# A hybrid attention and ConvFFN layer on one core: when the projections' weights are loaded, when a power is taken, and in which order the kernel begins

## The chip, the core and the metric

The kernel runs on one core of a Trainium2 chip. Its five instruction streams are those of TensorE (PE), VectorE (DVE), ScalarE (ACT), GpSimd (POOL) and SyncE (SP, which here only issues DMAs). Each takes its instructions in program order and waits on semaphores of the others. ACT issues a few DMAs of its own. The metric is device time in microseconds (us); the median of three runs is shown for the kernel before.

## What is computed

One layer over 1024 latent tokens and 256 context tokens of 1024 channels. Cut to what the change touches:

```python
mod = jax.nn.silu(c) @ w_mod[l] + b_mod[l]
shift1, scale1, gate1, shift2, scale2, gate2 = jnp.split(mod[:, None, :], N_MOD, axis=-1)
...
h = x * (1.0 + scale1) + shift1
...
proj = h @ w_in + b_in                   # q, k, v of two attentions, and 2048 gate columns
q_b = _rope_2d(_qk_rms(q_b, q_norm_g))   # t * (mean(t * t) + eps) ** -0.5 * g, then rotary
...
g_a, g_b = jnp.split(jax.nn.sigmoid(gate_logits), 2, axis=-1)
```

Behind this follow a windowed and a global attention, their merge, a layer norm, a convolutional feed-forward part and a second layer norm. The change leaves those as they are.

## The kernel before

**Arithmetic.** Every operand of a product is split into a high part (rounded to the type fp32r) and a low part (what rounding lost), and each product is three passes of PE: high by high, high by low, low by high (`mm3`, lines 88 to 91). A high part is a copy, on ACT as a rule (line 81, CAST in the trace); a low part is a subtraction, on DVE or POOL (line 86).

**The beginning (lines 199 to 278).** c is loaded as a row into all partitions (`spread_load`, 64 partitions on ACT's queue, 64 on SP's), and ACT takes its silu (`spread`, line 184). For each of eight channel tiles k, `load1` loads two 512 KB tiles of the transposed modulation weights (wm, for shift and scale), a raw 256 KB weight tile of the global queries (wr) and a 512 KB tile of x; line 192 (`mod`) multiplies wm by silu(c) and sums it on DVE, which gives a column of shift or scale. `modulate` then makes hh and hl, the parts of h, on ACT (lines 230 and 231, twice the same affine function) and DVE (line 237), and splits the next raw weights. PE multiplies tile k into eight accumulators, q1acc, in 24 products of 512 columns (lines 275 to 278). In each cycle of loads the raw weights come ahead of x.

**The rest of the projections (lines 656 to 832).** An order is written out by hand (GORD): 3 gates, the group qa (windowed queries of tokens 0 to 511), 4 gates, qb (the other tokens), 4 gates, ka (keys and values), 1 gate, kb, 4 gates. A gate is 48 products for 128 gate columns in two halves; a group runs over eight k, each with its own weight tile (12 products per k in qa and qb, 15 in ka and kb). The weights pass through three raw buffers (tile raw, RAWB): `fetch_raw` issues a load for each buffer counted free, `prefetch` splits them one step ahead, and in `prefetch` the last call is `fetch_raw` (lines 688 and 699), so raw loads are issued directly behind the splits that free the buffers. A load waits at the head of SP's queue until its buffer is really free, and what is behind it on SP waits as well.

Beside this, `mods` (line 718) spreads 48 more products of modulation rows over the half gates and the k steps: `fetch` issues the load of a row (wml0, wml1, ..., 512 KB, on SP) and line 192 multiplies it on DVE. The rows have a ring of four buffers (WRING), so the load of row n waits for the product of row n - 4.

`side_step` runs the queries' normalisation (`qpost`) in steps, one per half gate: s1 (a rotary table on POOL, squares on ACT), s1b (sums on DVE, line 330; then the power -0.5 on POOL, line 332, and its negative, line 370), an empty step (GAP), and s2 (rotary, lines 304 to 312, on DVE or POOL). The power's results pqs and nqs are read in the attention.

Up to the start of ka the order of all five streams is that of the program (`manual_schedule`, closed at line 785); from there on a scheduler orders them, and it also lifts a few small loads into the earlier part of SP's queue.

The rest of the kernel runs over 32 attention units, the merge, and the feed-forward part; PE is kept supplied there by orders and delays that the change does not touch.

Of the kernel before, what the change touches and what calls it, by code (L numbers as in the profile page):

```python
# [17 lines left out]
KT = 8  # L18
# [38 lines left out]
UE = "vector", "vector", "vector", "vector", "vector", "gpsimd", "gpsimd"  # L57
LN2_P = 2, 2, 2
GAP = 1
WRING = 4  # L60
LN1_S = slice(0, 512), slice(512, 768), slice(768, 1024)
VOFF = 0.0
# [6 lines left out]
def layer_kernel(  # L69
# [65 lines left out]
    def hput(*names):  # L135
        for n in names:
            hfree.append(hslot.pop(n))
# [8 lines left out]
    def acc_tile(name, dt=F32):  # L146
        return ps1.tile([P, 512], dt, tag="acc", name=name)
# [28 lines left out]
    def spread_load(src, n, engs):  # L176
        rows[n] = ht(f"row{n}")
        hput(f"row{n}")
        for m, eng in enumerate(engs):
            w = P // len(engs)  # L180
            eng.dma_start(rows[n][m * w:(m + 1) * w], src.partition_broadcast(w))
# [14 lines left out]
    Q = {}  # L196
    st1 = {}

    def load1(k):
        wm = []  # L200
        for j in (0, 1):
            w = tmp(f"wm{j}_{k}")
            nc.sync.dma_start(w, wmodT[j * 8 + k])
            wm.append(w)
        x = tmp(f"xr{k}")
        wr = raw(f"wr{k}")
        nc.sync.dma_start(wr, w_qb[k])
        for s in [slice(0, HALF), slice(HALF, T)] if k == 0 else [slice(0, T)]:
            nc.sync.dma_start(x[:, s], xT[k][:, s])
        st1[k] = wm, x, wr  # L210

    def product(j, k):
        col = j * 8 + k
        mod(st1[k][0][j], sc, bmc[:, col:col + 1], modc[:, col:col + 1])

    def modulate(k):
        wr = st1[k + 1][2] if k + 1 < KT else None
        if k == 0:
            w0.append(wsplit(st1[0][2], "qb0", "gpsimd"))
        elif k + 1 < KT:  # L220
            w0.append([ph1.tile([P, 512], R32, tag="wp", name=f"w{a}qb{k + 1}", bufs=8) for a in "hl"])
            nc.scalar.copy(w0[-1][0], wr)
        product(1, k)
# [4 lines left out]
        ss = (slice(0, HALF), slice(HALF, T)) if k == 0 else (slice(0, T),)  # L228
        for s in ss:
            nc.scalar.activation(hh[:, s], x[:, s], AF.Identity, bias=a, scale=b)  # L230
            nc.scalar.activation(x[:, s], x[:, s], AF.Identity, bias=a, scale=b)
        if k + 1 < KT:
            if k:
                nc.vector.tensor_tensor(out=w0[-1][1], in0=wr, in1=w0[-1][0].bitcast(F32), op=ALU.subtract)
            product(0, k + 1)
        for s in ss:
            nc.vector.tensor_tensor(out=hl[:, s], in0=x[:, s], in1=hh[:, s].bitcast(F32), op=ALU.subtract)
        if k == 0:
            w0.append(wsplit(wr, "qb1"))
        hT.append((hh, hl))  # L240

    loads = ctx.enter_context(ExitStack())
    E = mybir.EngineType
    loads.enter_context(tc.manual_schedule(engines={E.SP, E.PE, E.DVE, E.Activation, E.Pool}))
    spread_load(c_row, 0, (nc.scalar, nc.sync))
    nc.scalar.dma_start(bmc, bmod)
    load1(0)
    spread(sc, 0)
    nc.vector.tensor_scalar(out=bmc[:, 8:16], in0=bmc[:, 8:16], scalar1=1.0, scalar2=None, op0=ALU.add)
    for k in (1, 2):  # L250
        load1(k)
    acc = [acc_tile(f"q1acc{t}") for t in range(NT)]
    w0 = []
    product(0, 0)
    modulate(0)
# [69 lines left out]
    def rms_scale(x3, H, nm, sq, ss=None, square=True):  # L325
        if square:
# [4 lines left out]
        nc.vector.tensor_scalar(out=ss, in0=ss, scalar1=1.0 / HD, scalar2=QK_EPS, op0=ALU.mult, op1=ALU.add)  # L331
        nc.gpsimd.tensor_tensor(out=ss, in0=ss, in1=mhalf[:, 0:H], op=ALU.pow)
        return ss
# [17 lines left out]
    def qpost(br, t):  # L351
        q = qtile(br, t)
        q3 = q.rearrange("p (h d) -> p h d", d=HD)
        if br == 0:
            def r0():
                rope(nc.gpsimd if t % 3 == 2 else nc.vector, q, q, 8, ropec[:, t], ropes[:, t], f"q0_{t}")
            return [r0]
        st = {}

        def s1():  # L360
            st["tb"] = ph1.tile([P, 2, HD], F32, tag="tb", name=f"tbq{t}", bufs=4)
            gfold(st["tb"], 0, t, nc.gpsimd)
            rms_square(q3, sqq[0][:, t % 2])

        def s1b():
            rms_scale(q3, 8, f"q{t}", sqq[0][:, t % 2], pqs[:, t], False)
            if t == NT - 1:
                sqq.clear()
                hput("sqq")
            nc.gpsimd.tensor_scalar(out=nqs[:, t], in0=pqs[:, t], scalar1=-1.0, scalar2=0.0, op0=ALU.mult, op1=ALU.add)  # L370

        def s2():
            tb = st["tb"]
            rope(nc.gpsimd if t % 3 == 2 else nc.vector, q, q, 8, tb[:, 0], tb[:, 1], f"q1_{t}")
        return [s1, s1b] + [lambda: None] * GAP + [s2]

    sqq = [ht("sqq", (P, 2, 512))]
    for t in range(NT):
# [302 lines left out]
    def prefetch(gi, k):  # L681
        if gi == "g":
            hs = []
            for a in (0, 1):
                hs.append(wsplit(rawt.pop((gi, k, a))[0], f"g{k}_{a}", "gpsimd"))
                raws[1] += 1
            ready[gi, k] = hs
            fetch_raw()
            return
        nm, src, tiles = groups[gi]  # L690
        wr, cx = rawt.pop((gi, k, 0))
        w, c = wsplit(wr, f"{nm}{k}"), None
        raws[1] += 1
        if cx is not None:
            nc.scalar.activation(cx, cx, AF.Identity, bias=modx[:, k:k + 1], scale=modx[:, 8 + k:9 + k])
            c = [ph1.tile([P, NC], R32, tag="ch", name=f"c{a}{k}", bufs=4) for a in "hl"]
            split(cx, *c, nc.vector, nc.vector)
        ready[gi, k] = w, c
        fetch_raw()

    late = [(col, sc, modc[:, col:col + 1]) for col in range(16, 48)]
    late += [(col, scc, modx[:, col:col + 1]) for col in range(16)]
# [80 lines left out]
    for n, (gi, k) in enumerate(order):  # L783
        if (gi, k) == (0, 0):
            loads.close()
            bias_kv = bias_tile(b_kv, "bias_kv")
        while nxt < len(order) and sum(ahead[n:nxt + 1]) <= 8:
            prefetch(*order[nxt])
            nxt += 1
        if gi == "g":  # L790
            for hf in (0, 1):
                last = gate(k, hf)
                mods(3 * KT)
                if not turn[0]:
                    prepare()
                    nc.vector.tensor_scalar(out=bias_qa, in0=bias_qa, scalar1=0.125, scalar2=None, op0=ALU.mult)
# [1039 lines left out]
```

## Time and profile before

| | us |
|---|---|
| median of three runs (lowest, highest) | 1592.48 (1592.48, 1593.41) |
| the profiled execution | 1589.56 |
| its span, first to last instruction | 1587.8 |
| PE busy | 1533.4 |
| DVE, ACT, POOL busy | 1175.5, 813.9, 728.8 |
| mean granted clock of PE | 0.994 |

The span lies 1.8 us below the profiled execution's own time. A row of a timeline reads: start (us), duration (us), engine, line, operation, out<-in, count, and in brackets the idle time of that engine just before it and what ended it. SPq and ACTq are the DMA issues of SP and ACT; a row with a count merges several instructions. Waits read: total, times, longest.

### The profile page before, as it was taken

What the parts mean: (1) busy time and instruction counts of PE and PEld (TensorE: products, weight loads), DVE (VectorE), ACT (ScalarE), POOL (GpSimd) and SP (SyncE); (2) the same over time, 40 slices, a digit from 0 to 9 for tenths busy, and PEclk for the clock granted to TensorE, in tenths of its full rate; (3) what the DMA queues carried; (4) which work ended last, traced back from release to release, by engine and by line L of the source; (5) the groups of instructions that cost most, each with busy time, mean ns of one, the idle gap of its engine ahead of it and who ended that gap; (6) DMA issues with size and microseconds to landing.
All of it is one profiled execution on the core that took longest, in us unless ns stands there. A gap on an engine that the chain in (4) does not pass through costs nothing.

```text
span 1587.8 us, 22177 instructions
## 1 busy us (share of the span) xinstructions
PE 1533.4 (97%) x7748; PEld 1276.1 (80%) x7748; DVE 1175.5 (74%) x1767; ACT 813.9 (51%) x1450; POOL 728.8 (46%) x728
## 2 busy tenths in 40 slices
PE   7999899999999999999999999999999999999997
PEld 5888688878886887777788988888888888888887
DVE  6674876628888777888674778788888787647884
ACT  5322122448887667688531564444444444435552
POOL 0254422416667556665422453566667665021121
PEclk9999999999999999999999999999999999999999
DMA  9666663322236556531451222333334446996831
GB/s 368 235 220 208 223 233 126 116 84 65 64 103 158 139 128 144 119 72 39 144 180 57 80 81 93 107 107 106 107 107 116 112 118 177 362 277 205 257 107 54
DMA packets 112528, 230.00 MB, mean 145 GB/s; under 512 B 12992, under 2 KB 27840, under 8 KB 112320
## 3 DMA queue, kind: packets, MB, share of 16 engines
q1 hardware_dynamic: 97184, 199.72, 38.1%
q0 software_dynamic: 10400, 20.19, 8.3%
q10 hardware_dynamic: 4832, 8.68, 1.5%
q8 instruction: 61, 1.00, 0.3%
q14 instruction: 51, 0.42, 0.1%
HBM read 177.35 MB, written 65.86 MB: 153 GB/s over the span
## 4 chain that ended last, share of the span: by engine, by line
PE 80%; DVE 8%; ACT 4%; DMA 3%; POOL 3%; issue 2%; SPq 0%; DVEq 0%; ACTq 0%; POOLq 0%
PE ptr L576 5%; PE p L90 4%; PE p L91 4%; PE p L89 4%; PE b L91 3%; PE b L90 3%; PE b L89 3%; PE g L89 3%; PE g L91 3%; PE g L90 3%; PE s L459 2%; PE av L597 2%; PE d L89 2%; PE c L89 2%; PE a L89 2%
## 5 line engine op out<-in xcount | busy, mean ns | idle before, releaser
L586 DVE TENSOR_TENSOR ptl<-ptr,pth 128x512 fp32r<-128x512 f32 x188 | 124.8, 685 | 27.5 <-ACT pth L585 25.3
L576 PE MATMUL ptr<-ident,p 128*128 128x128 f32 x816 | 126.7, 278 | 10.0 <-DVE ptl L586 7.7
L585 ACT CAST pth<-ptr 128x512 fp32r<-128x512 f32 x188 | 106.5, 588 | 56.1 <-PE ptr L576 32.6
L86 DVE TENSOR_TENSOR ld<-rd,hd 128x1024 fp32r<-128x1024 f32 x77 | 94.9, 1250 | 50.4 <-ACT hd L81 48.3
L471 ACT ACTIVATE p<-p,nm 128x1024 f32<-128x1024 f32 (+2 forms) x128 | 125.4, 982 | 10.8 <-DVE p L504 10.0
L576 PEld LDWEIGHTS ptr<-ident,p 128*128 128x128 f32 x816 | 93.7, 140 | 40.1 <-DVE ptl L586 13.8
L81 ACT CAST hd<-rd 128x1024 fp32r<-128x1024 f32 x77 | 79.4, 1049 | 80.7 <-PE p L91 51.7
L597 PE MATMUL av<-pth,VT 128*128 128x512 f32 x236 | 104.6, 443 | 1.0 <-ACT avs L603 0.5
L89 PE MATMUL p<-hd 128*128 128x512 f32 x264 | 103.2, 391 | 0.0
L90 PE MATMUL p<-ld,hd 128*128 128x512 f32 x264 | 102.8, 389 | 0.0
L91 PE MATMUL p<-hd,ld 128*128 128x512 f32 x264 | 102.8, 389 | 0.0
L91 PE MATMUL g<-hh,wlg 128*128 128x512 f32 x256 | 99.8, 390 | 0.8 <-POOL wlg L86 0.8
L89 PE MATMUL g<-hh,whg 128*128 128x512 f32 x256 | 99.9, 390 | 0.0
L90 PE MATMUL g<-hl,whg 128*128 128x512 f32 x256 | 99.6, 389 | 0.0
L598 PE MATMUL av<-ptl,VT 128*128 128x512 f32 x236 | 97.7, 414 | 2.0 <-POOL ptl L86 1.8
L86 POOL TENSOR_TENSOR wlg<-wg,whg 128x512 fp32r<-128x512 f32 x32 | 42.7, 1346 | 114.5 <-ACT whg L81 110.5
L504 DVE TENSOR_SCALAR_CACHE_REDUCE p<-s,cvt,nmc 128x1024 f32<-128x1024 f32 x64 | 84.5, 1340 | 12.3 <-PE s L460 12.0
L459 PE MATMUL s<-KL,q 128*128 128x512 f32 (+2 forms) x192 | 76.0, 396 | 2.7 <-ACT p_x L471 2.0
L192 DVE CUSTOM_DVE_ANT_0 wml<-wml,sc,bmc 128x1024 f32<-128x1024 f32 x32 | 44.7, 1412 | 37.5 <-DMA wml<-in_wmodT_dram 37.5
L83 POOL TENSOR_SCALAR pth<-prw 128x512 fp32r<-128x512 f32 x48 | 30.9, 643 | 88.9 <-ACT prw L582 63.1
L460 PE MATMUL s<-KL,q 128*128 128x512 f32 (+2 forms) x192 | 71.6, 373 | 0.0
L81 ACT CAST wS<-s 128x512 fp32r<-128x512 f32 x76 | 45.7, 621 | 47.2 <-POOL s L1167 44.0
(429 smaller groups left out, 4940.5 us busy)
## 6 DMA issues: line engine op xcount, KB each, us to landing
wml<-in_wmodT_dram SPq DMA_DIRECT2D x48, 512.0 KB
ru<-in_w_up_dram SPq DMA_DIRECT2D x38, 512.0 KB
rd<-td SPq DMA_DIRECT2D x55, 256.0 KB
rd<-sd SPq DMA_DIRECT2D x44, 256.0 KB
rd<-in_w_dn_dram SPq DMA_DIRECT2D x33, 256.0 KB
wm<-in_wmodT_dram SPq DMA_DIRECT2D x16, 512.0 KB
wg<-in_w_g_dram SPq DMA_DIRECT2D x32, 256.0 KB
sgd<-sg ACTq DMA_DIRECT2D x32, 256.0 KB
```

Source lines behind the costliest of these rows:

```text
L81: nc.scalar.copy(hi, src)
L86: lo_eng.tensor_tensor(out=lo, in0=src, in1=hi.bitcast(F32), op=ALU.subtract)
L89: nc.tensor.matmul(ps, a[0], b[0], start=start, stop=False, skip_group_check=resumed)
L90: nc.tensor.matmul(ps, a[0], b[1], start=False, stop=False, skip_group_check=resumed)
L91: nc.tensor.matmul(ps, a[1], b[0], start=False, stop=stop, skip_group_check=resumed)
L459: nc.tensor.matmul(o, self.q[0][:, hs], ks, start=True, stop=False)
L471: nc.scalar.activation(p, s, AF.Exp, bias=nm[:, h:h + 1], scale=scale, accum_out=sm[:, h:h + 1])
L576: nc.tensor.transpose(tr[:, h * P:(h + 1) * P], self.pslice(h, n), ident)
L585: nc.scalar.copy(hi, tr)
L586: nc.vector.tensor_tensor(out=lo, in0=tr, in1=hi.bitcast(F32), op=ALU.subtract)
L597: nc.tensor.matmul(self.av, v, hi, start=first, stop=False)
L598: nc.tensor.matmul(self.av, v, lo, start=False, stop=self.left == 0)
```

## The change

1. Raw weights in the gates: `prefetch` no longer calls `fetch_raw` at its end. In a gate the call stands behind the first half's products and `side_step`, in a k step of a group ahead of `prefetch`; where a raw tile isn't there when it is to be split, it is fetched then.
2. The power: s1b ends with the sums; the power and its negative move to a new step s1c in the place of the empty step.
3. The beginning: bmc (the modulation bias, 24 KB) is now the first load on ACT's queue and the second half of c_row the second; a silu of one column of ones (into negsink, which is set later) is put ahead of everything ACT computes, and with it the load of ACT's function table; x of tile 0 is loaded around its raw weights, and from then on raw weights are loaded one tile ahead, behind x; the high part of tile 0's weights is a copy on DVE behind the first two products, no longer on ACT; DVE takes the second product of tile 1 between the two halves of hl0; PE gets 28 products of ones, 128 by 128 by 128 in f32, into an accumulator ahead of its work.

```diff
+    def load_w(k):
+        wr1[k] = wr = raw(f"wr{k}")
+        nc.sync.dma_start(wr, w_qb[k])
...
-        wr = raw(f"wr{k}")
-        nc.sync.dma_start(wr, w_qb[k])
-        for s in [slice(0, HALF), slice(HALF, T)] if k == 0 else [slice(0, T)]:
-            nc.sync.dma_start(x[:, s], xT[k][:, s])
-        st1[k] = wm, x, wr
+        if k == 0:
+            nc.sync.dma_start(x[:, 0:HALF], xT[k][:, 0:HALF])
+            load_w(0)
+            nc.sync.dma_start(x[:, HALF:T], xT[k][:, HALF:T])
+        else:
+            nc.sync.dma_start(x, xT[k])
+        if k + 1 < KT:
+            load_w(k + 1)
+        st1[k] = wm, x
...
         if k == 0:
-            w0.append(wsplit(wr, "qb1"))
+            product(1, 0)
+            w = [ph1.tile([P, 512], R32, tag="wp", name=f"w{a}qb0", bufs=8) for a in "hl"]
+            split(wr1[0], *w, nc.vector, nc.gpsimd)
+            w0.append(w)
+            high(slice(0, HALF))
+            high(slice(HALF, T))
+            product(0, 1)
+            low(slice(0, HALF))
+            product(1, 1)
+            low(slice(HALF, T))
+            w0.append(wsplit(wr1[1], "qb1"))
...
-    spread_load(c_row, 0, (nc.scalar, nc.sync))
     nc.scalar.dma_start(bmc, bmod)
+    spread_load(c_row, 0, (nc.sync, nc.scalar))
+    nc.scalar.activation(negsink[:, 0:1], onec, AF.Silu)
     load1(0)
...
+    for _ in range(NWARM):
+        nc.tensor.matmul(acc[-1][:, 0:P], onesf, onesf, start=True, stop=True)
...
         def s1b():
-            rms_scale(q3, 8, f"q{t}", sqq[0][:, t % 2], pqs[:, t], False)
+            rms_scale(q3, 8, f"q{t}", sqq[0][:, t % 2], pqs[:, t], True)
...
+        def s1c():
+            rms_power(pqs[:, t], 8)
             nc.gpsimd.tensor_scalar(out=nqs[:, t], in0=pqs[:, t], scalar1=-1.0, scalar2=0.0, op0=ALU.mult, op1=ALU.add)
...
-        return [s1, s1b] + [lambda: None] * GAP + [s2]
+        return [s1, s1b, s1c, s2]
...
             for a in (0, 1):
+                if (gi, k, a) not in rawt:
+                    fetch_raw()
                 hs.append(wsplit(rawt.pop((gi, k, a))[0], f"g{k}_{a}", "gpsimd"))
                 raws[1] += 1
             ready[gi, k] = hs
-            fetch_raw()
             return
         nm, src, tiles = groups[gi]
+        if (gi, k, 0) not in rawt:
+            fetch_raw()
...
         ready[gi, k] = w, c
-        fetch_raw()
...
+        if gi != "g":
+            fetch_raw()
         while nxt < len(order) and sum(ahead[n:nxt + 1]) <= 8:
...
                 side_step()
+                if hf == 0:
+                    fetch_raw()
             continue
```

How the change moves instructions, at three places. First SP's queue in the last gate ahead of qb and in qb itself. wqb0 to wqb7 are the raw weights of qb's eight k steps, wml rows those of `mods`. Before:

```order
L675 DMA wqb1_1207<-in_w_qa_dram 128x512
L675 DMA wqb2_1209<-in_w_qa_dram 128x512
L714 DMA wml22_1239<-in_wmodT_dram 128x1024
L714 DMA wml23_1274<-in_wmodT_dram 128x1024
L714 DMA wml24_1277<-in_wmodT_dram 128x1024
L675 DMA wqb3_1294<-in_w_qa_dram 128x512
L675 DMA wqb4_1300<-in_w_qa_dram 128x512
L714 DMA wml25_1330<-in_wmodT_dram 128x1024
L714 DMA wml26_1333<-in_wmodT_dram 128x1024
```

And after:

```order
L751 DMA wml22_1262<-in_wmodT_dram 128x1024
L710 DMA wqb1_1272<-in_w_qa_dram 128x512
L710 DMA wqb2_1274<-in_w_qa_dram 128x512
L751 DMA wml23_1303<-in_wmodT_dram 128x1024
L751 DMA wml24_1306<-in_wmodT_dram 128x1024
L751 DMA wml25_1353<-in_wmodT_dram 128x1024
L751 DMA wml26_1356<-in_wmodT_dram 128x1024
L710 DMA wqb3_1366<-in_w_qa_dram 128x512
L710 DMA wqb4_1368<-in_w_qa_dram 128x512
```

One wml row (wml22) has moved ahead of wqb1 and wqb2, and two (wml25 and wml26) ahead of wqb3 and wqb4.

Second POOL's queue in the four gates between qa and qb. wlg5_0 is the low part of the first half of gate 5's weights, `cvt<-cvt,mhalf` the power, the TENSOR_SCALAR behind it its negative, tbq a rotary table of the query tile of that number. Before:

```order
L315 TENSOR_TENSOR tbq4_1060<-ropet_137,gcol_138 128x64
L320 TENSOR_TENSOR tbq4_1060<-ropet_137,gcol_138 128x2x16 x2
L332 TENSOR_TENSOR cvt_69<-cvt_69,mhalf_72 128x8
L370 TENSOR_SCALAR cvt_69<-cvt_69 128x8
L86 TENSOR_TENSOR wlg5_0_1106<-wg5_0_979,whg5_0_1105 128x512
L86 TENSOR_TENSOR wlg5_1_1110<-wg5_1_1022,whg5_1_1109 128x512
L315 TENSOR_TENSOR tbq5_1151<-ropet_137,gcol_138 128x64
L320 TENSOR_TENSOR tbq5_1151<-ropet_137,gcol_138 128x2x16 x2
L332 TENSOR_TENSOR cvt_69<-cvt_69,mhalf_72 128x8
L370 TENSOR_SCALAR cvt_69<-cvt_69 128x8
L86 TENSOR_TENSOR wlg6_0_1200<-wg6_0_1024,whg6_0_1199 128x512
```

And after:

```order
L343 TENSOR_TENSOR tbq4_1085<-ropet_137,gcol_138 128x64
L348 TENSOR_TENSOR tbq4_1085<-ropet_137,gcol_138 128x2x16 x2
L87 TENSOR_TENSOR wlg5_0_1133<-wg5_0_1021,whg5_0_1132 128x512
L87 TENSOR_TENSOR wlg5_1_1137<-wg5_1_1090,whg5_1_1136 128x512
L365 TENSOR_TENSOR cvt_69<-cvt_69,mhalf_72 128x8
L405 TENSOR_SCALAR cvt_69<-cvt_69 128x8
L343 TENSOR_TENSOR tbq5_1176<-ropet_137,gcol_138 128x64
L348 TENSOR_TENSOR tbq5_1176<-ropet_137,gcol_138 128x2x16 x2
L87 TENSOR_TENSOR wlg6_0_1227<-wg6_0_1092,whg6_0_1226 128x512
```

The power and its negative have moved from ahead of a gate's low parts to behind them; between the low parts of gates 5 and 6 there now stands the power of the query tile before.

Third ACT's queue at the start of the program. row0 is c's row, 64 of its partitions; whqb0 the high part of tile 0's weights. Before:

```order
L181 DMA row0_146<-in_c_row_dram 64x1024
L246 DMA bmc_61<-in_bmod_dram 128x48
L184 ACT_TABLE_LOAD
L184 ACTIVATE sc_142<-row0_146 128x1024
L81 CAST whqb0_186<-wr0_155 128x512
L230 ACTIVATE hh0_191<-xr0_154,modc_60 128x512
```

And after:

```order
L270 DMA bmc_61<-in_bmod_dram 128x48
L182 DMA row0_147<-in_c_row_dram 64x1024
L272 ACT_TABLE_LOAD
L272 ACTIVATE negsink_63<-onec_70 128x1
L185 ACTIVATE sc_142<-row0_147 128x1024
L241 ACTIVATE hh0_217<-xr0_155,modc_60 128x512
```

The two loads have changed places, the table load no longer has a row ahead of it that it must wait for, and the cast has left this queue.

More of the change, by code (lines that the diff above doesn't have):

```diff
@@ L59 @@
 GAP = 1
+NWARM = 28
 WRING = 4
@@ L197, in layer_kernel @@
     st1 = {}
+    def load_w(k):
+        wr1[k] = wr = raw(f"wr{k}")
+        nc.sync.dma_start(wr, w_qb[k])
+    wr1 = {}
     def load1(k):
@@ L216, in modulate @@
     def modulate(k):
[L217 to L223, printed above, removed]
+        last = k + 1 == KT
+        if k:
+            if not last:
+                w0.append([ph1.tile([P, 512], R32, tag="wp", name=f"w{a}qb{k + 1}", bufs=8) for a in "hl"])
+                nc.scalar.copy(w0[-1][0], wr1[k + 1])
+            if k > 1:
+                product(1, k)
         hh = hTp.tile([P, T], R32, tag="hT", name=f"hh{k}", bufs=16)
@@ L227, in modulate, with high, low @@
         x = st1[k][1]
-        ss = (slice(0, HALF), slice(HALF, T)) if k == 0 else (slice(0, T),)
-        for s in ss:
+        def high(s):
             nc.scalar.activation(hh[:, s], x[:, s], AF.Identity, bias=a, scale=b)
             nc.scalar.activation(x[:, s], x[:, s], AF.Identity, bias=a, scale=b)
[L232 to L236, printed above, removed]
+        def low(s):
             nc.vector.tensor_tensor(out=hl[:, s], in0=x[:, s], in1=hh[:, s].bitcast(F32), op=ALU.subtract)
         if k == 0:
-            w0.append(wsplit(wr, "qb1"))
+            product(1, 0)
[9 more added lines that the diff above has]
+            w0.append(wsplit(wr1[1], "qb1"))
+        else:
+            high(slice(0, T))
+            if not last:
+                nc.vector.tensor_tensor(out=w0[-1][1], in0=wr1[k + 1], in1=w0[-1][0].bitcast(F32), op=ALU.subtract)
+                product(0, k + 1)
+            low(slice(0, T))
         hT.append((hh, hl))
@@ L323, in rms_square, with rms_scale @@
         nc.scalar.activation(sq.rearrange("p (h d) -> p h d", d=HD), x3, AF.Square)
-    def rms_scale(x3, H, nm, sq, ss=None, square=True):
-        if square:
+    def rms_scale(x3, H, nm, sq, ss=None, late=False):
+        if not late:
             rms_square(x3, sq)
@@ L331, in rms_scale, with rms_power @@
         nc.vector.tensor_scalar(out=ss, in0=ss, scalar1=1.0 / HD, scalar2=QK_EPS, op0=ALU.mult, op1=ALU.add)
+        if not late:
+            rms_power(ss, H)
+        return ss
+    def rms_power(ss, H):
         nc.gpsimd.tensor_tensor(out=ss, in0=ss, in1=mhalf[:, 0:H], op=ALU.pow)
-        return ss
     def rms_apply(x3, H, ss):
```

## The prediction

> **What bounds the kernel now.** I read the page first, then the waits of TensorE (PE) over the projections (0 to 400 us), and then the timelines of the engines around the two places where those waits sit. The page:
>
> ```profile
> span 1587.8 us, 22177 instructions
> PE 1533.4 (97%) x7748; PEld 1276.1 (80%) x7748; DVE 1175.5 (74%) x1767; ACT 813.9 (51%) x1450; POOL 728.8 (46%) x728
> ```
>
> PE is busy for 97% of the span, so a change that adds no PE work can only give back time in which PE waits, or runs slowly, where the change reaches. These are the waits of PE in the first 400 us (total, times, longest):
>
> ```profile
> PE q1acc L275 <- ACT hh L230: 11.4, 2, 10.7
> PE accqb L90 <- DVE wlqb L86: 5.9, 1, 5.9
> PE g L91 <- POOL wlg L86: 0.8, 1, 0.8
> ```
>
> The reader is to see three places: the beginning (10.7 + 0.7), one stop of 5.9 in the group qb, one of 0.8 in the gate ahead of it. First the stop in qb on PE's timeline:
>
> ```profile
> 163.31 0.39 PE L89 MATMUL accqb<-whqb,hh 128*128 128x512 f32 x1
> 169.61 0.80 PE L90 MATMUL accqb<-wlqb,hh 128*128 128x512 f32 x1 [5.91 <-DVE wlqb L86]
> 170.20 0.63 PE L91 MATMUL accqb<-whqb,hl 128*128 128x512 f32 x1
> 170.62 0.63 PE L89 MATMUL accqb<-whqb,hh 128*128 128x512 f32 x1
> ...
> 174.12 0.39 PE L89 MATMUL accqb<-whqb,hh 128*128 128x512 f32 x1
> ...
> 179.56 0.39 PE L89 MATMUL accqb<-whqb,hh 128*128 128x512 f32 x1
> ```
>
> From 174.12 to 179.56 PE issues 24 products, one each 0.227 us. Behind the stop they come every 0.42 to 0.43 (170.20 to 170.62). Between 163.31 and 174.12 lie 12 issues, which at 0.227 take 2.7; they took 10.8. The stop thus costs **8.1 us**: the wait and the slow stretch behind it.
>
> Why is wlqb late? VectorE (DVE), then SyncE's queue (SP):
>
> ```profile
> 144.16 1.28 DVE L192 CUSTOM_DVE_ANT_0 wml<-wml,sc,bmc 128x1024 f32<-128x1024 f32 x1
> 164.65 1.28 DVE L192 CUSTOM_DVE_ANT_0 wml<-wml,sc,bmc 128x1024 f32<-128x1024 f32 x1 [3.67 <-DMA wml<-in_wmodT_dram]
> 168.87 1.29 DVE L86 TENSOR_TENSOR wlqb<-wqb,whqb 128x512 fp32r<-128x512 f32 x2
> ```
>
> ```profile
> 147.27 1.57 SPq L675 DMA_DIRECT2D wqb<-in_w_qa_dram  x2
> 148.94 2.49 SPq L714 DMA_DIRECT2D wml<-in_wmodT_dram  x3
> 157.31 0.93 SPq L675 DMA_DIRECT2D wqb<-in_w_qa_dram  x2
> 158.29 1.37 SPq L714 DMA_DIRECT2D wml<-in_wmodT_dram  x3
> ```
>
> DVE stood still for the row wml25, issued at 158.29; only then came its product, the rotary step and the sums (3.0 us, from the product's end at 165.9 to 168.87), and last the two splits PE was waiting for. wml25 was issued so late because wqb3 and wqb4 stood ahead of it (157.31), and those wait for a free raw buffer. The pair before them (147.27) waited for GpSimd (POOL), as did the gate that lost 0.8:
>
> ```profile
> 136.33 1.14 ACT L81 CAST whg<-wg 128x512 fp32r<-128x512 f32 x2 [0.45 <-DMA wml<-in_wmodT_dram]
> 159.23 2.08 ACT L81 CAST whqb<-wqb 128x512 fp32r<-128x512 f32 x3 [0.47 <-ACT sg L746]
> ```
>
> ```profile
> 143.13 2.60 POOL L332 TENSOR_TENSOR cvt<-cvt,mhalf 128x8 f32<-128x8 f32 x1 [11.16 <-DVE cvt L331]
> 145.98 2.52 POOL L86 TENSOR_TENSOR wlg<-wg,whg 128x512 fp32r<-128x512 f32 x2
> ```
>
> The high parts of that gate's weights were ready from 136.33 on, but in POOL's order the power stood ahead of the low parts, and it stood 11.16 us for sums on DVE.
>
> **The change, the power and the raw weights.** With the power one step later, POOL reaches the low parts of gate 6 when their high parts are there: they start by about 137.5 instead of 145.98, so the 0.8 goes, and the raw buffers that wqb1 and wqb2 need come free about 8 us sooner. In SP's new order wml25 stands ahead of wqb3 and wqb4. It then waits only for its ring buffer, which the product of wml21 frees (144.16 + 1.28 = 145.4). From issue to use wml25 took 164.65 - 158.29 = 6.4, so I put it at 152 at the latest, 12 us sooner. DVE then needs three products (3.7), the 3.0 of rotary step and sums and a few small operations moved in behind them; counted from 152 that ends near 157. The bound is then the cast at 159.23: split at about 160.4, and PE wants it at 163.5 (163.31 + 0.23). About 3 us of cover is left, and 8.1 + 0.8 = **8.9 us** come back. From both sides: nothing, if another row is as late there; 8.9, if all goes.
>
> What the change adds is that raw loads now queue behind one or two rows of wml on SP, and a row of wml waits for DVE's product four rows earlier. Behind such a wait stand raw weights, and for them ScalarE (ACT) with its casts, then PE. As the raw buffers come free no later than before, I cost this at nothing; without that cover a late raw weight would cost PE what it costs above, a few us and the slow stretch. The four small loads that SP issued among the first wml rows (bias_kv, two of cx, the conv bias) come a few rows later, ahead of a raw load that must wait for its buffer anyway: nothing. The power's own results are wanted only in the attention.
>
> **The change, the beginning.** The first 27 us:
>
> ```profile
> 0.73 0.57 ACTq L181 DMA_DIRECT2D row<-in_c_row_dram  x1
> 0.86 0.17 DVE L116 MEMSET onesf<- 128x128 f32 x1
> 1.34 0.85 ACTq L246 DMA_DIRECT2D bmc<-in_bmod_dram  x1
> 4.61 1.28 ACT L184 ACT_TABLE_LOAD   x1 [4.61 <-DMA row<-in_c_row_dram]
> 5.93 1.06 ACT L184 ACTIVATE sc<-row 128x1024 f32<-128x1024 f32 x1
> 7.16 0.17 DVE L249 TENSOR_SCALAR bmc<-bmc 128x8 f32<-128x8 f32 x1 [6.12 <-DMA bmc<-in_bmod_dram]
> 7.29 1.28 DVE L192 CUSTOM_DVE_ANT_0 wm<-wm,sc,bmc 128x1024 f32<-128x1024 f32 x1
> 9.68 1.26 POOL L86 TENSOR_TENSOR wlqb<-wr,whqb 128x512 fp32r<-128x512 f32 x1 [9.25 <-ACT whqb L81]
> 9.82 0.81 ACT L230 ACTIVATE hh<-xr,modc 128x512 fp32r<-128x512 f32 x1 [0.23 <-DVE modc L192]
> 10.69 0.79 PE L275 MATMUL q1acc<-whqb,hh 128*128 128x512 f32 x1 [10.69 <-ACT hh L230]
> ...
> 16.76 0.40 PE L275 MATMUL q1acc<-whqb,hh 128*128 128x512 f32 x1
> 18.08 0.62 ACT L222 CAST whqb<-wr 128x512 fp32r<-128x512 f32 x1 [3.89 <-DMA wr<-in_w_qb_dram]
> 19.89 0.50 PE L275 MATMUL q1acc<-whqb,hh 128*128 128x512 f32 x1 [0.70 <-ACT hh L230]
> ...
> 22.60 0.62 ACT L222 CAST whqb<-wr 128x512 fp32r<-128x512 f32 x1 [1.48 <-DMA wr<-in_w_qb_dram]
> ```
>
> ```profile
> 26.19 0.39 PE L275 MATMUL q1acc<-whqb,hh 128*128 128x512 f32 x1
> ```
>
> ```profile
> 62.55 0.41 DVE L796 TENSOR_SCALAR bias_qa<-bias_qa 128x512 f32<-128x512 f32 x1
> ```
>
> ```profile
> 1576.27 0.69 PE L1658 MATMUL zt<-pr,zz 128*128 128x128 f32 x4
> 1576.80 0.50 PE L1663 MATMUL stl<-onec,pr 128*128 128x1 f32 x4
> ```
>
> PE starts at 10.69 and runs slowly until 16.76; channel tile 1 starts at 19.89, held by the cast at 18.08, which waits for wr2 and stands ahead of hh1 on ACT; tile 2 starts at 26.19. From there on PE no longer waits in this stage, so 26.19 is what has to move.
>
> The table load leaves the path. But the second half of c_row is now issued on ACT behind bmc. As first of that queue it let ACT go on at 5.93 or just before; the second of the queue, bmc, landed at 7.16. SP's half, issued at the same time, landed at 4.61, 1.3 sooner than ACT's: that is what a half costs. So the second half, as second, lands between 4.7 (bounded below by SP's half, if bmc costs nothing) and 7.16 + 1.3 = 8.4. I take 8.4, since the place in the queue is that of bmc. Then: silu to 9.5 (1.06), the first hh 2.5 behind the start of the first product, as before (7.29 to 9.82), at 12.0, and PE's first product 0.87 behind hh (9.82 to 10.69), at 12.85. The cast of wr0 is now on DVE behind the two products (11.9), 0.41 by the nearest row: 12.3; POOL's low part 1.26: 13.6; PE's second product at 13.65. On the good side, wr2 is loaded ahead of tile 2's two 512 KB rows; a tile's 1.8 MB take 4.5 (18.08 to 22.60, the casts that wait for wr2 and wr3), so wr2 comes 2.6 sooner, at 15.5, and tile 1 no longer waits for it.
>
> The 28 products can start when onesf is set, at about 1.1. Four of that shape take 0.53 at full speed (1576.27 to 1576.80), 0.13 each, so 0.25 at the slow rate: they end between 1.1 + 3.7 and 1.1 + 7.0, by 8.1. Then PE idles for 4.7 us or more until 12.85. The wait of 5.91 above was long enough for the slow rate; I take it that this one is too. [...]
>
> Slow stretches lasted 4.5 and 6.1 here (169.61 to 174.12, 10.69 to 16.76). From 12.85 that is to 17.4 or 18.9: of the 23 products from 13.65 on, 9 to 12 take 0.42, the rest 0.227, so tile 0 ends at 20.6 to 21.3, and with tile 1's 24 x 0.227 = 5.44 the next tile begins at 26.0 to 26.7, against 26.19. I take **0** for the beginning. The other edits cost nothing: the products write an accumulator whose first real product starts it anew, and the extra silu runs while the rows load.
>
> **The sum.** 8.1 + 0.8 + 0 = 8.9. The profiled execution took 1589.56 (span 1587.8 and 1.8 around it), 2.9 below the median of 1592.48; against its own time 1589.56 - 8.9 = 1580.7, span 1578.9; against the median **1583.6**.
>
> **The rivals.**
> 1. *The beginning gains too.* The clock stays up through the gap, or c_row lands early. With the clock up: 13.65 + 23 x 0.227 = 18.9, and 24.3 for the next tile, 1.9 gained. With c_row landing as early as before as well, tile 1 is held by its loads, which come 2.6 sooner: 2.6 gained. That gives 1592.48 - 8.9 - 1.9 = 1581.7, or 1581.0. [...] Against: the queue's place of c_row. Chance 0.30.
> 2. *The stop shrinks or moves.* Less waiting on one row shows the next: a raw weight behind wml makes PE wait 2 to 6 somewhere in qa, qb or ka. Result 8.9 less 3 to 7: 1586.6 to 1590.6, mostly about 1587.5. The cover in qb is only 3 us. Chance 0.13.
> 3. *It does not do what it says.* DVE's order around wlqb is the same as before (product, rotary step, sums, splits); if its row is as late as ever, the 8.1 stays and only 0.8 goes: 1591.7. Against: the row's place on SP has changed. Chance 0.07.
> 4. *Slower.* In the first k/v group (ka), scheduled freely, the scaling of the context now stands on ACT ahead of the third cast and waits for products whose rows were pushed back on SP; if each of the six remaining weights there waits for a row (6.4 from issue to use, against 15 x 0.227 = 3.4 of PE work per weight), that is 6 x 3.0 = 18 and a slow stretch (8.1 - 5.9 = 2.2 above), so -8.9 + 20 = +11: 1603.6; it is slower as soon as more than 2 us are lost on each. Against: before, nothing in that group waited. Chance 0.05.
>
> The forecast has 0.45. **Chances:** 0.2% is about what a measurement of this kernel can tell from no change (3.2 us: 1589.3 to 1595.7). Faster: forecast, rival 1 and nearly all of rival 2: 0.87. Same: rival 3 and a little of 2: 0.08. Slower: 0.05. **Range:** forecast (-0.5 to +0.2 for the beginning), rival 1 down to 1580.0 with its last tenths, and the greater part of rival 2: 1580.0 to 1588.0; some 0.16 is left out.
>
> **What would show it.** Right: no wait of PE on wlqb or wlg above 0.5 us, no slow stretch in qb, POOL's low parts directly behind their casts, wml25 landed before DVE wants it; PE's first real product near 12.9, slow again, and tile 2 begun near 26. Wrong: PE's first product before 11 or at full speed; a wait of PE on wlqb that stays; a new wait on wqa, wka or whka; a time above 1588.

## The result and the profile after

| | before | after |
|---|---|---|
| median (lowest to highest) | 1592.24 (1590.44 to 1593.41), 6 runs | 1579.37 (1577.02 to 1581.23), 6 runs |
| profiled execution, its span | 1589.56, 1587.8 | 1578.46, 1576.7 |

The changed kernel is faster: the ratio of the times is 0.992, 95% interval 0.9907 to 0.9933. The forecast was 1583.6, its range 1580.0 to 1588.0; the result lies 4.2 below the one and 0.6 below the other. By the medians 12.9 us are gained, by the two profiled executions 11.1.

The page of after:

```profile
span 1576.7 us, 22297 instructions
PE 1538.4 (98%) x7804; PEld 1283.1 (81%) x7804; DVE 1199.0 (76%) x1768; ACT 813.8 (52%) x1450; POOL 740.2 (47%) x728
```

PE is busy for 5 us more than before (the products of ones take 9) in a span that is 11 us shorter. The waits of PE of after over the first 400 us, those on the tiles of which the prediction spoke (total, times, longest):

```profile
PE q1acc L280 <- DVE mhalf L118: 1.1, 1, 1.1
PE q1acc L306 <- DVE hl L245: 0.9, 1, 0.9
PE q1acc L304 <- POOL wlqb L87: 0.4, 1, 0.4
PE q1acc L303 <- ACT hh L241: 0.2, 1, 0.2
```

The wait of 5.9 on wlqb in qb and that of 0.8 on wlg are gone; where PE stood 10.7 ahead of its first product, it now works on the products of ones and stands 1.1 and 0.2. How the gain builds up is read from where a stage begins. A tile's rows give the first and the last start of a line's products; here qb and then ka, of before:

```profile
L89 PE MATMUL accqb<-whqb,hh x32: 388/389/632, 157.9 to 187.0; 128*128 128x512 f32 x32
L89 PE MATMUL accka<-whka,hh x40: 389/389/389, 231.2 to 257.8; 128*128 128x512 f32 x40
```

and of after:

```profile
L90 PE MATMUL accqb<-whqb,hh x32: 389/389/389, 154.1 to 175.2; 128*128 128x512 f32 x32
L90 PE MATMUL accka<-whka,hh x40: 389/389/389, 219.4 to 245.9; 128*128 128x512 f32 x40
```

PE reaches qb 3.8 earlier and ka 11.8 earlier: 8.0 come from qb (the slow products, 632 ns and more, are gone too). The start of the first gate, the stage behind the beginning, divides the 3.8. Of before and of after:

```profile
58.83 0.39 PE L89 MATMUL g<-hh,whg 128*128 128x512 f32 x1
```

```profile
56.18 0.39 PE L90 MATMUL g<-hh,whg 128*128 128x512 f32 x1
```

So the beginning gives **2.65**, the gates up to qb **1.1**, qb **8.0**: 11.8. At the end of the span 11.1 are left. Part of the 0.7 in between is the clock behind a wait that both kernels have (2.9 on DVE, near 947 in before and 936 in after). Windows of before and of after (span, busy times, PE's granted clock third from the end):

```profile
930.00:1000.00 70.00, 66.68 (x355) 58.15 (x354) 61.63 (x67) 37.12 (x50) 33.27 (x24) 0.98 0.25 83
```

```profile
930.00:1000.00 70.00, 67.12 (x326) 57.67 (x325) 58.52 (x55) 35.76 (x45) 36.18 (x25) 0.95 0.26 88
```

The change does not reach there, and the same wait of 2.9 left the clock of this stretch at 0.95 in the profiles of no_power and no_warm (mean over their spans 0.994 and 0.995) and at 1.00 in those of c_row_first, warm36 and old_loads (0.997, 0.998 and 0.997; five kernels of the experiments below).

In the gate ahead of qb, ACT's cast and POOL's low parts of after:

```profile
133.68 1.14 ACT L82 CAST whg<-wg 128x512 fp32r<-128x512 f32 x2 [0.45 <-ACT sg L783]
```

```profile
134.38 3.53 POOL L87 TENSOR_TENSOR wlg<-wg,whg 128x512 fp32r<-128x512 f32 x2 [4.93 <-ACT whg L82]
```

The low parts begin 0.7 behind the start of their casts; before, it was 9.65 (136.33 to 145.98). SP and DVE of after:

```profile
135.70 2.56 SPq L710 DMA_DIRECT2D wqb<-in_w_qa_dram  x2
138.35 1.83 SPq L751 DMA_DIRECT2D wml<-in_wmodT_dram  x4
145.94 0.93 SPq L710 DMA_DIRECT2D wqb<-in_w_qa_dram  x2
```

```profile
146.43 1.28 DVE L193 CUSTOM_DVE_ANT_0 wml<-wml,sc,bmc 128x1024 f32<-128x1024 f32 x1
...
148.90 1.28 DVE L193 CUSTOM_DVE_ANT_0 wml<-wml,sc,bmc 128x1024 f32<-128x1024 f32 x1
...
156.10 1.29 DVE L87 TENSOR_TENSOR wlqb<-wqb,whqb 128x512 fp32r<-128x512 f32 x2 [2.45 <-ACT whqb L82]
```

wml25, the third of the rows between the two pairs of splits, is multiplied at 148.90 (164.65 before), without a wait for its DMA. The splits begin at 156.10, behind the cast and no longer behind a row, and PE wants wlqb2 at 154.1 + 24 x 0.227 = 159.5.

The beginning of after:

```profile
1.08 9.23 PE L280 MATMUL q1acc<-onesf 128*128 128x128 f32 x56 [1.08 <-DVE mhalf L118]
...
2.58 0.17 DVE L275 TENSOR_SCALAR bmc<-bmc 128x8 f32<-128x8 f32 x1 [1.54 <-DMA bmc<-in_bmod_dram]
...
5.61 1.06 ACT L185 ACTIVATE sc<-row 128x1024 f32<-128x1024 f32 x1 [2.37 <-DMA row<-in_c_row_dram]
...
10.50 0.50 PE L303 MATMUL q1acc<-whqb,hh 128*128 128x512 f32 x1 [0.19 <-ACT hh L241]
11.40 0.50 PE L304 MATMUL q1acc<-wlqb,hh 128*128 128x512 f32 x1 [0.39 <-POOL wlqb L87]
...
15.41 0.62 ACT L232 CAST whqb<-wr 128x512 fp32r<-128x512 f32 x1 [2.05 <-DMA wr<-in_w_qb_dram]
...
17.89 0.39 PE L303 MATMUL q1acc<-whqb,hh 128*128 128x512 f32 x1
...
23.54 0.39 PE L303 MATMUL q1acc<-whqb,hh 128*128 128x512 f32 x1
```

c_row's second half is there at 5.61, not at 8.4. Its silu ends at 6.67, and the first product on DVE begins at 7.04, when its wm has landed. The 28 products of ones are 56 records (two for each product) and last until 10.31, not 8.1. The first real product starts 0.19 behind them, at 10.50 (10.69 before), and takes 0.50, against 0.79 before. Tile 1 starts at 17.89 instead of 19.89, tile 2 at 23.54 instead of 26.19.

### The profile page after: what moved, and what is told of

Read it like the earlier page. It is cut to its first block, busy times and chain, and to the rows that moved or that the text cites. A ratio compares the mean times of both kernels' runs of the same rounds, so it can differ in the third digit from the quotient of the medians.

```text
span 1576.7 us, 22297 instructions
## 1 busy us (share of the span) xinstructions
PE 1538.4 (98%) x7804; PEld 1283.1 (81%) x7804; DVE 1199.0 (76%) x1768; ACT 813.8 (52%) x1450; POOL 740.2 (47%) x728
## 4 chain that ended last, share of the span: by engine, by line
PE 87%; DVE 5%; ACT 3%; issue 2%; POOL 1%; DMA 0%; SPq 0%; DVEq 0%; ACTq 0%; POOLq 0%
PE ptr L611 5%; PE p L90 4%; PE p L91 4%; PE p L92 4%; PE g L90 4%; PE g L92 4%; PE g L91 4%; PE b L92 3%; PE b L91 3%; PE b L90 3%; PE av L632 2%; PE s L494 2%; PE av L633 2%; PE d L92 2%; PE c L92 2%; PE a L92 2%
## 5 line engine op out<-in xcount | busy, mean ns | idle before, releaser
L611 PE MATMUL ptr<-ident,p 128*128 128x128 f32 x816 | 126.8, 278 | 10.5 <-DVE ptl L621 8.2
L506 ACT ACTIVATE p<-p,nm 128x1024 f32<-128x1024 f32 (+2 forms) x128 | 125.3, 981 | 10.7 <-DVE p L539 10.0
L539 DVE TENSOR_SCALAR_CACHE_REDUCE p<-s,cvt,nmc 128x1024 f32<-128x1024 f32 x64 | 84.4, 1339 | 12.1 <-PE s L495 11.8
L783 ACT ACTIVATE sg<-g,bgc 128x512 f32<-128x512 f32 x32 | 22.0, 687 | 97.0 <-PE g L92 92.0
L82 ACT CAST wA<-ru 128x512 fp32r<-128x512 f32 x57 | 35.5, 623 | 67.8 <-PE d L92 36.2
```

What stands on the lines that cost most here:

```text
L82: nc.scalar.copy(hi, src)
L506: nc.scalar.activation(p, s, AF.Exp, bias=nm[:, h:h + 1], scale=scale, accum_out=sm[:, h:h + 1])
L611: nc.tensor.transpose(tr[:, h * P:(h + 1) * P], self.pslice(h, n), ident)
```

## The experiments

The theory: three separate gains (beginning, gate, stop in qb) that add up. Its rivals: the pieces need each other; one of the two edits in the projections does the work alone; the products of ones, or the loads, do it alone in the beginning. The first gate's start is a better measure of the beginning than the time, since executions of one kernel spread over 2 to 5 us. It has a spread of its own: five profiles with the old beginning (before, rest_only, raw_only, power_only, rows_ahead3) have it between 58.83 and 59.78, three with the new one (after, begin_only, no_power) between 56.18 and 56.48.

| kernel | median (lowest to highest), runs | ratio to before, 95% | first gate |
|---|---|---|---|
| begin_only | 1588.05 (1584.37 to 1589.81), 11 | 0.9974, 0.9965 to 0.9983 | 56.48 |
| rest_only | 1582.39 (1580.47 to 1585.02), 5 | 0.9944, 0.9931 to 0.9956 | 59.08 |
| raw_only | 1582.07 (1581.63 to 1583.70), 5 | 0.9942, 0.9928 to 0.9955 | 59.78 |
| power_only | 1582.52 (1582.12 to 1583.88), 5 | 0.9944, 0.9931 to 0.9956 | 58.92 |
| rows_ahead3 | 1581.63 (1580.23 to 1584.11), 5 | 0.9940, 0.9928 to 0.9953 | 59.26 |
| no_power | 1578.16 (1577.21 to 1580.13), 5 | 0.9916, 0.9902 to 0.9929 | 56.23 |
| no_warm | 1578.64 (1577.35 to 1580.45), 5 | 0.9926, 0.9914 to 0.9939 | 57.52 |
| warm14 | 1579.14 (1578.44 to 1581.43), 5 | 0.9931, 0.9919 to 0.9943 | 57.18 |
| old_loads | 1581.66 (1581.52 to 1582.47), 5 | 0.9944, 0.9931 to 0.9958 | 59.54 |
| c_row_first | 1578.42 (1577.23 to 1579.92), 5 | 0.9923, 0.9910 to 0.9935 | 56.38 |
| warm36 | 1580.30 (1578.80 to 1581.20), 5 | 0.9927, 0.9915 to 0.9940 | 56.24 |

Before ran beside them with medians of 1591.84 (15 runs; begin_only, rest_only, raw_only, power_only), 1591.50 (9; no_warm, warm14, old_loads, c_row_first) and 1591.65 (9; rows_ahead3, warm36, no_power).

**begin_only**: before with the new beginning.

```diff
-    spread_load(c_row, 0, (nc.scalar, nc.sync))
     nc.scalar.dma_start(bmc, bmod)
+    spread_load(c_row, 0, (nc.sync, nc.scalar))
+    nc.scalar.activation(negsink[:, 0:1], onec, AF.Silu)
...
+    for _ in range(NWARM):
+        nc.tensor.matmul(acc[-1][:, 0:P], onesf, onesf, start=True, stop=True)
...
```

> Before with the new beginning alone (load order, early table load, 28 products of ones). Theory, three separate gains that add up (beginning 2.7, gate 1.1, stop 8.1 by the starts of PE's products in the two traces): about 2.7 less than before, 1589.5; channel tile 2 starts near 23.5 instead of 26.19, the wait on wlqb in qb stays at 5 to 7. Rival, the pieces hang together (the earlier start only lengthens the stop in qb, which ends when DVE lets it): tile 2 near 23.5 too, but the wait in qb grows by 2 to 3 and the time is that of before, 1592.2.

The first gate begins 2.35 earlier than in before. The waits of PE behind it:

```profile
PE accqb L91 <- DVE wlqb L87: 5.5, 1, 5.5
PE g L92 <- POOL wlg L87: 1.4, 1, 1.4
```

The wait in qb did not grow by the lead; the two waits together are 6.9, against 6.7 before. The time is 3.8 below before's. The profile shows less: 1.9 of the lead is left where ka begins (229.3), and the profiled execution, 1589.81, is the slowest of the eleven. In it the clock did not hold at the start:

```profile
1.08 8.24 PE L280 MATMUL q1acc<-onesf 128*128 128x128 f32 x56 [1.08 <-DVE mhalf L118]
10.56 0.50 PE L303 MATMUL q1acc<-whqb,hh 128*128 128x512 f32 x1 [1.24 <-ACT hh L241]
11.44 0.73 PE L304 MATMUL q1acc<-wlqb,hh 128*128 128x512 f32 x1 [0.37 <-POOL wlqb L87]
11.96 0.63 PE L303 MATMUL q1acc<-whqb,hh 128*128 128x512 f32 x1
```

The same 28 products took 8.24 here and 9.23 in after, so I take it that their fast rate set in earlier; they left a gap of 1.24, and from 11.4 on products took 0.63 and more (granted clock 0.51 from 11.6 to 15.0). The first gate begins 0.3 later than in after (56.48 against 56.18).

**rest_only**: after with before's beginning.

```diff
-    nc.scalar.dma_start(bmc, bmod)
-    spread_load(c_row, 0, (nc.sync, nc.scalar))
-    nc.scalar.activation(negsink[:, 0:1], onec, AF.Silu)
+    spread_load(c_row, 0, (nc.scalar, nc.sync))
+    nc.scalar.dma_start(bmc, bmod)
...
-    for _ in range(NWARM):
-        nc.tensor.matmul(acc[-1][:, 0:P], onesf, onesf, start=True, stop=True)
...
```

> The change with the old beginning (raw weights moved and power moved, nothing else). Theory of separate gains: 1.1 + 8.1 = 9.2 less than before, 1583.0; tile 2 at 26.2, no wait of PE on wlqb or wlg. Rival, the new loads need the early start (they queue behind rows of wml, and the lead of 2.7 us hides it): a wait of 1 to 3 in qb and about 1585 to 1586.

9.5 below before, with no wait on wlqb or wlg: the projections' part does not need the earlier start. 9.45 + 3.79 = 13.2 against 12.9 for the whole: the pieces add up within the spread. By the starts of ka it is 8.9 (222.3) + 1.9 against 11.8.

**raw_only**: before with the moved raw loads alone, the power at its old place.

```diff
             ready[gi, k] = hs
-            fetch_raw()
             return
...
+        if gi != "g":
+            fetch_raw()
...
+                if hf == 0:
+                    fetch_raw()
```

> Before with the moved raw loads alone; the power keeps its old place. Theory, either of the two edits is enough for the stop: wml25 no longer stands behind wqb3 and wqb4 on SP, so the 8.1 go or nearly (PE waits at most 2 on wlqb); the low parts of gate 6 still stand behind the power, so the 0.8 stays: 6 to 8.1 less than before, 1584 to 1586. Rival A, the power is the root: the raw buffers come free as late as before, PE still waits 4 or more on wlqb, 1590 to 1592.

**power_only**: before with the power one step later alone.

```diff
-            rms_scale(q3, 8, f"q{t}", sqq[0][:, t % 2], pqs[:, t], False)
+            rms_scale(q3, 8, f"q{t}", sqq[0][:, t % 2], pqs[:, t], True)
...
+        def s1c():
+            rms_power(pqs[:, t], 8)
...
-        return [s1, s1b] + [lambda: None] * GAP + [s2]
+        return [s1, s1b, s1c, s2]
```

> Before with the power one step later alone; raw loads are issued at their old places. Theory, either of the two edits is enough for the stop: the low parts of gate 6 start by 138, wqb1 and wqb2 get their buffers 8 us sooner, wqb3 and wqb4 follow, and wml25 behind them comes in time: 8 to 9.2 less than before, 1583 to 1584. Rival B, the order on SP is the root: wml25 still stands behind wqb3 and wqb4, only the wait of the gate goes and PE still waits 4 or more on wlqb: 1591.

Either edit alone gives all: 1582.07 and 1582.52 beside 1582.39 for both (against before 9.8, 9.3 and 9.5), and in neither does PE wait on wlqb or wlg. So raw_only gave more than I expected (I had left the 0.8 in). The waits of DVE for rows and of POOL for the sums, between 100 and 180 us, show why. Before:

```profile
DVE wml L192 <- DMA wml<-in_wmodT_dram: 26.5, 5, 9.7
```

```profile
POOL cvt L332 <- DVE cvt L331: 34.9, 5, 11.2
```

raw_only:

```profile
DVE wml L193 <- DMA wml<-in_wmodT_dram: 3.4, 4, 1.7
```

```profile
POOL cvt L333 <- DVE cvt L332: 16.8, 4, 7.7
```

```profile
139.52 2.56 SPq L676 DMA_DIRECT2D wqb<-in_w_qa_dram  x2
```

power_only:

```profile
DVE wml L192 <- DMA wml<-in_wmodT_dram: 13.4, 5, 6.8
```

```profile
POOL cvt L337 <- DVE cvt L331: 13.4, 3, 6.7
```

Before, there was a ring of waits: the power on POOL waits for sums, the sums stand on DVE behind products that wait for rows, the rows stand on SP behind raw weights, these wait for buffers, and the buffers come free by the low parts that stand on POOL behind the power. A delay went round from gate to gate. raw_only takes the rows out from behind the raw weights, so DVE hardly waits and POOL's wait falls too; power_only takes the low parts out from behind the power, so SP goes on sooner: wqb1 and wqb2 are issued at 138.73 in power_only, at 139.52 in raw_only and at 147.27 before.

```profile
138.73 1.76 SPq L682 DMA_DIRECT2D wqb<-in_w_qa_dram  x2
```

That one cut ends the stop would be so in a plain chain of waits too. That the chain closes is read from the waits: where only the raw loads moved, POOL's wait for sums ahead of the power halved (34.9 to 16.8), and where only the power moved, DVE's wait for rows halved (26.5 to 13.4).

**rows_ahead3**: a cut at a third place, before with one row more fetched ahead.

```diff
-    for _ in range(WRING // 2):
+    for _ in range(WRING // 2 + 1):
         fetch()
```

> Before with the rows of wml fetched three ahead instead of two; raw loads, power and beginning as before. Theory, a loop: the power waits for sums on DVE, the sums stand behind products that wait for rows of wml, the rows stand on SP behind raw weights, and these wait for buffers that POOL's low parts behind the power free; a cut at any link ends it. With this third cut (wml25 now ahead of wqb3 and wqb4, wml22 ahead of wqb1 and wqb2) the waits of DVE of 8.5 and 3.7 and the stop go: 8 to 9.2 less than before, 1582.5 to 1584. Rival, the raw buffers themselves are short and the rows only follow: PE still waits 4 or more on wlqb, 1589 to 1591.

10.0 below before, the stop and the gate's wait gone. DVE's waits for rows:

```profile
DVE wml L192 <- DMA wml<-in_wmodT_dram: 9.2, 4, 7.0
```

Before, wml22 was waited for 8.45 and wml25 for 3.67; now no row from 135 us on is waited for more than 0.54. One wait of 7.0, at 134.56, stayed and cost PE nothing. With the three raw buffers as before the stop is gone, so the ring, not a shortage of raw buffers, made it.

**no_power**: after with the power back at its old place.

```diff
-        return [s1, s1b, s1c, s2]
+        return [s1, s1b] + [lambda: None] * GAP + [s2]
...
```

> After with the power back at its old place (raw weights moved and the new beginning stay). Theory, one cut of the loop is enough: the time of after, 1579.4, no wait of PE on wlqb or wlg above 0.5. Rival, with the earlier start the second cut is needed: POOL stands several us for the sums ahead of the low parts, a wait of PE of 0.8 to 6 in the gate or in qb, 1580.2 to 1587.

1578.16, no wait of PE on wlqb or wlg: with the raw loads moved, the power's new place is worth nothing that can be measured. The same follows from rest_only beside raw_only.

**no_warm**: after with NWARM = 0.

```diff
-NWARM = 28
+NWARM = 0
```

> After without the 28 products of ones. Theory, the products hold the clock up: PE's first real product still at 10.5, but at half speed for about 6 us, as in before (10.69 to 16.76, where 24 products took 8.5 instead of 7.4 in after): tile 2 starts at 24.5 to 25.0 instead of 23.54, the time 1.0 to 1.5 above after, 1580.4 to 1580.9. Rival, the loads alone set the beginning and PE's speed is hidden in waits for DVE and ACT: tile 2 at 23.5 to 23.8 and 1579.4 to 1579.7.

**warm14**: after with NWARM = 14.

```diff
-NWARM = 28
+NWARM = 14
```

> After with 14 products of ones in place of 28. By the rates in after's trace (0.427 each at half speed, 0.222 from 6.8 on) they end at 7.1, 3.4 before the first real product at 10.5. [...] Rival, the step of my forecast (a gap of some us, as in qb, is enough): half speed from 10.5 for about 6 us as without any products, tile 2 at 24.5 to 25.0, 1580.4 to 1580.9.

PE's beginning in warm14, a window of it (granted clock third from the end), and its first gate:

```profile
1.08 5.85 PE L280 MATMUL q1acc<-onesf 128*128 128x128 f32 x28 [1.08 <-DVE mhalf L118]
10.50 0.79 PE L303 MATMUL q1acc<-whqb,hh 128*128 128x512 f32 x1 [3.57 <-ACT hh L241]
11.38 0.80 PE L304 MATMUL q1acc<-wlqb,hh 128*128 128x512 f32 x1
```

```profile
9.70:16.50 6.80, 5.91 (x13) 4.33 (x14) 4.60 (x9) 4.66 (x7) 1.27 (x1) 0.50 1.04 408
```

```profile
57.18 0.39 PE L90 MATMUL g<-hh,whg 128*128 128x512 f32 x1
```

and the first gate of no_warm:

```profile
57.52 0.39 PE L90 MATMUL g<-hh,whg 128*128 128x512 f32 x1
```

A gap of 3.57 brought the clock down (0.50 from 9.7, within the gap, to 16.5), as the rival (my forecast's step) had it; 14 products are worth little more than none (0.3). The 28 are worth 1.0 to 1.3 at the first gate. In the times this does not show (1578.64 and 1579.14 beside 1579.37): the expected 1.0 to 1.5 above after fell inside the spread.

**old_loads**: after with each tile's raw weights ahead of its own x.

```diff
-        if k == 0:
-            nc.sync.dma_start(x[:, 0:HALF], xT[k][:, 0:HALF])
-            load_w(0)
-            nc.sync.dma_start(x[:, HALF:T], xT[k][:, HALF:T])
-        else:
-            nc.sync.dma_start(x, xT[k])
-        if k + 1 < KT:
-            load_w(k + 1)
+        load_w(k)
+        for s in [slice(0, HALF), slice(HALF, T)] if k == 0 else [slice(0, T)]:
+            nc.sync.dma_start(x[:, s], xT[k][:, s])
```

> After with the raw weights loaded as before (each tile's own, ahead of its x), all else new. Theory, the earlier wr2 is what frees tile 1: its cast again at 18.1 and tile 1 at 19.5 to 19.9 instead of 17.89, tile 2 at 25.0 to 25.4, 1.5 to 1.9 above after, 1580.9 to 1581.3. Rival, with PE at full speed from the start the order of loads is worth nothing: tile 2 at 23.5 to 23.8, 1579.4 to 1579.7.

```profile
17.98 0.62 ACT L227 CAST whqb<-wr 128x512 fp32r<-128x512 f32 x1 [3.90 <-DMA wr<-in_w_qb_dram]
18.50 1.24 ACT L236 ACTIVATE hh<-xr,modc 128x1024 fp32r<-128x1024 f32 x1
19.79 0.80 PE L298 MATMUL q1acc<-whqb,hh 128*128 128x512 f32 x1 [2.42 <-ACT hh L236]
20.39 0.63 PE L299 MATMUL q1acc<-wlqb,hh 128*128 128x512 f32 x1
```

wr2's cast is back at 17.98 and tile 1 at 19.79, as expected. But more is lost than the wait: behind a gap of 2.42 the granted clock was 0.50 from 19.7 to 23.1 (products of 0.63), tile 2 began at 26.90 (expected: 25.0 to 25.4), and the first gate begins at 59.54, 3.4 later than in after and where kernels with the old beginning have it. So the products of ones without the earlier weights gain nothing here, since PE only reaches the late weights sooner; all the rest of the new beginning without the products gains 1.3 (no_warm, 58.83 - 57.52). What the early table load and the copy on DVE give by themselves was not run.

**c_row_first**: after with the first loads in before's order.

```diff
-    nc.scalar.dma_start(bmc, bmod)
-    spread_load(c_row, 0, (nc.sync, nc.scalar))
+    spread_load(c_row, 0, (nc.scalar, nc.sync))
+    nc.scalar.dma_start(bmc, bmod)
```

> After with the first loads as before (half of c_row on each queue first, the modulation bias bmc second on ACT's queue). Theory, the place behind a big load delays only bmc: c_row lands by 5.9, bmc at 7.2, the first product starts at 7.3 instead of 7.04; 0.3 above after or nothing, 1579.4 to 1579.7. Rival, the step of my forecast (the second place costs 1.3 or more whatever stands first): then c_row, now first, lands 1.3 or more sooner than 5.6, by 4.3, and bmc at 7.2 sets the start, also 7.3; the two differ in c_row's landing, not in the time.

```profile
5.67 1.06 ACT L185 ACTIVATE sc<-row 128x1024 f32<-128x1024 f32 x1 [2.22 <-DMA row<-in_c_row_dram]
5.77 0.17 DVE L275 TENSOR_SCALAR bmc<-bmc 128x8 f32<-128x8 f32 x1 [4.73 <-DMA bmc<-in_bmod_dram]
```

c_row is there at 5.67, as when it is second (5.61): so the theory had it, and not the rival. bmc, second again as in before, is there at 5.77, not at the 7.2 that both expected: the place on ACT's queue showed no fixed price. The first gate lies 0.2 behind that of after, as much as kernels with the same beginning differ by. Why bmc came at 7.16 in before's profile stays open.

**warm36**: after with NWARM = 36.

```diff
-NWARM = 28
+NWARM = 36
```

> After with 36 products of ones in place of 28. [...] Rival, the longer row of products holds up the first tile: the gate begins 0.8 to 1.6 later, 1580.2 to 1581.

```profile
1.08 10.82 PE L280 MATMUL q1acc<-onesf 128*128 128x128 f32 x72 [1.08 <-DVE mhalf L118]
11.66 0.48 PE L303 MATMUL q1acc<-whqb,hh 128*128 128x512 f32 x1
11.97 0.40 PE L304 MATMUL q1acc<-wlqb,hh 128*128 128x512 f32 x1
```

No gap ahead of the real products and no slow one among them (0.48 and 0.40, beside 0.79 and 0.80 in warm14; granted clock 1.00 over the first 30 us, against 0.89 there). The real work starts 1.2 later and loses nothing by the first gate (56.24 against 56.18; the rival had it 0.8 to 1.6 later). The median, 1580.30, is 0.9 above after's, with overlapping intervals: no gain that can be measured.

No version beats after beyond its spread. The plainest of those that reach it is no_power.

## Why the prediction was wrong in size

**Right: the stop, 8.1.** 8.0 came back in qb. wml25 was used at 148.90 (forecast: there by 152), and the cover ahead of wlqb2 is 159.5 - 156.8 = 2.7 (forecast: about 3). That nothing else moved into its place held; rivals 2, 3 and 4 did not happen.

**Right in kind, too small: the gate, 0.8.** 1.1 came back.

**Incomplete: the cause of the stop.** The prediction named every link but credited both edits together and did not see that the links close a ring. raw_only, power_only and rows_ahead3 show that any one cut is enough.

**Wrong: "I take 0 for the beginning".** 2.65 came back. Two terms of that step failed:
- *c_row at 8.4, which is 7.16 + 1.3.* It was there at 5.61. I read a price of the second place from bmc's 7.16; c_row_first put bmc at the same place and it came by 5.77. The 1.3, from 4.61 to 5.93, is the time of ACT's own table load (1.28), so those rows show only the latest time at which ACT's half can have landed. The first real product was at 10.50, not 12.85.
- *The products of ones, 0.13 or 0.25 each.* They took 9.23 / 28 = 0.33 on average. The row I used (zt, four records in 0.53) is only two products: line 1658 runs once for each of two tiles of tokens, and each product is two records, as those of ones are. Two in 0.53 are 0.27 each. With 0.33 they last until 10.31.

With both, the gap was 0.19 and not 4.7, and the clock stayed up (1.00 from 10.5 to 16.5, with products of 0.39 to 0.50). That it did is in part the luck of this execution: begin_only, with the same beginning, lost it at 11.6 (0.51 to 15.0). The step in between, that a gap of a few us brings it down, was an estimate from the one wait of 5.91; it held where it was tried (warm14 at 3.57, old_loads at 2.42, both 0.50), but not for every gap of that length (the wait of 2.9 near 936, 1.00 in three profiles). How long a gap has to be, no run shows. The loads' part was right (wr2's cast at 15.41, forecast 15.5; tile 1 no longer held), but the forecast let the late start eat it.

**Rival 1 is what happened**, with 2.65 for its 1.9 to 2.6. With 2.65 in place of 0 the forecast would have been 1580.9, still 1.6 above the result. By the profiled executions: 8.9 forecast, 11.1 measured; 2.65 + 0.3 came on top, 0.7 was lost later. That makes 2.2 of the 4.2 by which the forecast missed. The other 2.0 are in setting the gain against the median: before's profiled execution (1589.56) lies 2.7 below the median of its 6 runs, after's (1578.46) only 0.9 below its own, and before's median itself came out 0.2 lower than the one I started from. The range's low end allowed for none of this spread.

## What to carry to other kernels

- When a stop is traced back through four queues, look whether the last link waits for the first. In this ring one cut was enough, and the second edit beside it bought nothing that could be measured; test each alone.
- Put a load where the next use wants it before keeping the clock up ahead of it: a PE that runs faster into a late load waits there, and the wait can take the clock down again (old_loads: a wait of 2.42, then a granted clock of 0.50).
- Price an operation from rows of the same form, and find in the program how many operations a row's count is: the four records of the zt row were two products.

## What the runs showed of the hardware

- **No one length of gap divides those that took the clock down from the others.** In begin_only gaps of 1.24 and 0.37 within 2.1 us were enough (then a granted clock of 0.51 from 11.6 to 15.0); in after 0.19, 0.39 and 0.85 were not (1.00 from 10.5 to 16.5). 2.42 alone was (old_loads, 0.50 from 19.7 to 23.1), and 2.05 in raw_only (0.50 from 20.7 to 24.1), whose first gate is the latest of those with the old beginning. The same length does not always do it: the wait of 2.9 near 936 left the clock at 1.00 in three profiles and at 0.95 in three.
- **The first products were slow, and the granted clock of the profile does not show it.** It reads 1.00 in before from 10.6 to 16.8, where products of 512 columns took mostly 0.63 (0.39 from 16.99 on), and 1.00 in no_warm over the first 30 us, where they took 0.63 to 0.80 from 10.58 on. A product of ones in f32, 128 by 128 by 128, took 5.85 / 14 = 0.42 among the first (warm14), and the 8 more of warm36 took 10.82 - 9.23 = 1.6, or about 0.2 each.
- **The same instructions did not take the same time in each execution**: the same 28 products took 9.23 in after and 8.24 in begin_only, whose beginning is the same.
